# Every two-input operation outside the top-k on VectorE, none of them on GpSimd, in a three-layer fp32 model kernel

## The chip, the core and the metric

One core of one Trainium2 chip runs the whole program in one launch. The time is the device time of one execution in microseconds (us). The kernel before was run three times: 2065.59, 2051.45 and 2052.27 us, median 2052.27. Engines are named as in the profile: PE is TensorE's matrix multiplication, PEld its weight loads, DVE is VectorE, ACT ScalarE, POOL GpSimd, SP the engine whose queue carries the weight transfers.

## The reference, cut to what matters

256 tokens of width 1024 go through one block of three branches with a mixture of experts behind it, and then through two layers of four branches, each with a feed-forward network behind it.

```
# block 1
h = rmsnorm(x, g_mix);  proj = h @ w_in
q_a, k_a, v_a, x_l, gate_l, q_m, gates = split(proj)
attn_out = windowed_gqa(rope(q_a), rope(k_a), v_a, sink)
xc       = conv over 4 tokens of x_l;  lru_out = bidir_rglru(xc, ...) * gelu(gate_l)
            # a = exp(log_a);  bx = sqrt(1 - a*a) * (i * xc);  two scans
mem_out  = memory_cross_attention(q_m, rmsnorm(mem, g_mem) @ w_mem_kv)
merged   = sum over the 3 branches of sigmoid(gates) * (branch @ p)
x = x + merged @ w_out
x = x + peer_ffn(rmsnorm(x, g_ffn))          # scores, two top-16, experts
# two layers, each
h = rms_norm(x, norm1_g);  z = h @ w_in
y0 = retention(z[..])          # q and k rotated: q*cos + turned(q)*sin
y1 = conformer_conv(z[..])     # 31 taps over the tokens, layer norm, silu
y2 = spatial_gating(z[..])     # gelu, layer norm (*g, +b), (w_s * mask) @ v + b_s, times u
y3 = swa_attention(z[..])
x = x + (sum over the 4 of sigmoid(gate) * (y @ w_branch)) @ w_out
x = x + ffn(rms_norm(x, norm2_g))
# at the end rmsnorm with g_final for block 1's part; all in float32
```

## The kernel before, in words

**Weights.** All weights are packed in one stream, in the order of use. A slot of the stream is 8 blocks of 128x128. `Stream._slot` (lines 77 to 101) takes the next slot: for every second one SP issues a transfer of 16 blocks into one of two buffers (`raw`), ACT writes the high half of the slot (`whi`, line 93), and DVE subtracts it from the weights, which gives the low half (`wlo`, line 96). There are 677 slots; in the stretch of the top-k, 59 of the subtractions run on POOL (`pool_share`). Slots have three buffers, so the halves can run at most some two slots ahead of PE. The scheduler gives these operations a high priority.

**Products.** Each block feeds three matmuls (`mm3`, lines 178 to 180, and `mm3a`, lines 184 to 186, where the activations stand still): high by high, high by low, low by high. An activation tile is cut in the same way by `split` (lines 188 to 196: high half by ACT on line 191, low half on line 192).

**The steps that the change touches.** `norm_split` multiplies eight pieces of 128x256 by the norm's factor (`nh`, line 312) and splits each; the low half `hl` goes to POOL for pieces 2, 4 and 6. It is used by six norms on the main path and by the norm of the memory (its names in the trace: `t<-nh,t`). The conv over four tokens (lines 466 to 475) has six pieces whose low halves POOL makes (`t<-t,t`). `lru` squares `lA` (line 564) and multiplies `lX` by `lV` (line 572) on POOL. `gated` (lines 611 to 637) adds a branch for each of eight column groups: a gate product (`gth`, line 634) on DVE, then the addition to `mg` (line 635), on POOL for the middle branches and on DVE for the last. The rotations of the retention end with an addition on POOL (line 1308), the spatial gating with the addition of line 1402 and the product of line 1415, and its weights are masked on POOL (line 1388).

**What sets the order.** Beside the stream of matmuls run background steps (attention, the conv, the recurrence, the retention, the gating). They are generators that are moved on by one step with each pair of blocks of the stream; their matmuls stand between the others. The scheduler places every instruction by its own estimate of times, once, when the program is built. On the chip each engine then works through its fixed list in order: an instruction that waits holds back all behind it on the same engine. So a waiting DVE instruction holds back the next `wlo`, and a late `wlo` holds back PE. The 31 taps of the conv in the two layers (line 1160, `t<-up,hw,t`, 120 for a layer) are filled in after `wlo` operations.

Of the kernel before, what the change touches and what calls it, by code (L numbers as in the profile page):

```python
# [19 lines left out]
P = 128  # L20
# [112 lines left out]
class Core:  # L133
# [174 lines left out]
    def norm_split(self, x, g, rb, hi, lo):  # L308
        nc = self.nc
        for k in range(KD):  # L310
            h = self.scr("nh")
            nc.vector.scalar_tensor_tensor(out=h, in0=x[:, k, :], scalar=g[:, k:k + 1], in1=rb,
                                           op0=ALU.mult, op1=ALU.mult)
            last = self.split(hi[:, k, :], lo[:, k, :], h, eng=nc.vector if k in (0, 1, 3, 5, 7) else nc.gpsimd)
        return last

    def residual(self, w, nk, hi, lo, raw, g):
# [103 lines left out]
    def block1(self):  # L421
        tc, nc, a, ws = self.tc, self.nc, self.a, self.ws
        with ExitStack() as st:
# [42 lines left out]
            def conv():  # L466
                for j in range(6):
                    nc.vector.tensor_scalar(out=xc[:, j, :], in0=xl[:, j, 0:S], scalar1=cw[:, j:j + 1],
                                            scalar2=cb[:, j:j + 1], op0=ALU.mult, op1=ALU.add)
                    for i in range(1, 4):  # L470
                        nc.vector.scalar_tensor_tensor(out=xc[:, j, :], in0=xl[:, j, i:i + S],
                                                       scalar=cw[:, i * 6 + j:i * 6 + j + 1], in1=xc[:, j, :],
                                                       op0=ALU.mult, op1=ALU.add)
                    self.split(xch[:, j, :], xcl[:, j, :], xc[:, j, :], eng=nc.gpsimd)
                    yield 1
            t_conv = self.add(conv())

# [63 lines left out]
            def lru():  # L541
                for j in range(0, 6, 2):
                    A = p.tile([P, 2, 2, S], F32, tag="lA", name="lA", bufs=1)
                    V = p.tile([P, 2, 2, S], F32, tag="lV", name="lV", bufs=1)
                    X = p.tile([P, 2, 2, S], F32, tag="lX", name="lX", bufs=1)
                    for d in range(2):
                        for m in range(2):
                            ps = self.mm.tile([P, 2, S], F32, tag="mm", name="mm")
                            for g in range(2):
                                wh, wl = ws.blks(("lru", 0, 0), d * 6 + j + m, g)  # L550
                                self.mm3(ps[:, g, :], wh, wl, xch[:, j + m, :], xcl[:, j + m, :], True, True)
                            i = d * 6 + j + m
                            col = slice(i, i + 1)
                            th = p.tile([P, 2, S], F32, tag="b2", name="lth", bufs=3)
                            nc.scalar.activation(out=th[:, 0, :], in_=ps[:, 0, :], func=AF.Tanh, scale=0.5,
                                                 bias=self.hbr[:, col])
                            nc.scalar.activation(out=th[:, 1, :], in_=ps[:, 1, :], func=AF.Tanh, scale=0.5,
                                                 bias=self.hbi[:, col])
                            nc.scalar.activation(out=A[:, d, m, :], in_=th[:, 0, :], func=AF.Exp,
                                                 scale=self.nhc[:, col], bias=self.nhc[:, col])  # L560
                            nc.scalar.activation(out=th[:, 0, :], in_=th[:, 0, :], func=AF.Tanh, scale=self.hc[:, col],
                                                 bias=self.hc[:, col])
                            v = V[:, d, m, :]
                            nc.gpsimd.tensor_tensor(out=v, in0=A[:, d, m, :], in1=A[:, d, m, :], op=ALU.mult)
                            nc.vector.scalar_tensor_tensor(out=v, in0=v, scalar=1.0, in1=th[:, 0, :],
                                                           op0=ALU.add, op1=ALU.mult)
                            nc.vector.scalar_tensor_tensor(out=X[:, d, m, :], in0=th[:, 1, :], scalar=1.0,
                                                           in1=xc[:, j + m, :], op0=ALU.add, op1=ALU.mult)
                        yield LRU_PACE
                    for d in range(2):  # L570
                        nc.scalar.activation(out=V[:, d], in_=V[:, d], func=AF.Sqrt, scale=0.25, bias=self.tiny)
                        nc.gpsimd.tensor_tensor(out=X[:, d], in0=X[:, d], in1=V[:, d], op=ALU.mult)
                    yield 2
                    for d in range(2):
                        rev = slice(None, None, -1) if d else slice(None)
                        for m in range(2):
                            nc.vector.tensor_tensor_scan(out=V[:, d, m, rev], data0=A[:, d, m, rev],
                                                         data1=X[:, d, m, rev], initial=0.0, op0=ALU.mult, op1=ALU.add)
                    nc.vector.tensor_tensor(out=V[:, 0], in0=V[:, 0], in1=V[:, 1], op=ALU.add)
                    nc.vector.tensor_tensor(out=V[:, 0], in0=V[:, 0], in1=gl[:, j:j + 2, :], op=ALU.mult)  # L580
                    if j == 0:
                        self.dump("lru", V[:, 0, 0, :])
                    self.split(lh[:, j:j + 2, :], ll[:, j:j + 2, :], V[:, 0])
                    yield 1
# [28 lines left out]
    def gated(self, wg, wp, nk, bh, bl, mg, gh, gl, hgb, first, last, tasks):  # L613

        nc, ws = self.nc, self.ws
        for c in range(KD):
            pg = self.mm.tile([P, S], F32, tag="mm", name="pg")
            for k in range(KD):
                wh, wl = ws.blks(wg, k, c)
                self.mm3(pg, wh, wl, self.hh[:, k, :], self.hl[:, k, :], k == 0, k == KD - 1)  # L620
            th = self.scr("gth")
            nc.scalar.activation(out=th, in_=pg, func=AF.Tanh, scale=0.5,
                                 bias=hgb[:, c:c + 1] if hgb is not None else 0.0)
            if c == 0:
                self.finish(*tasks)
            pp = self.mm.tile([P, S], F32, tag="mm", name="pp")
            for k in range(nk):
                wh, wl = ws.blks(wp, k, c)
                self.mm3(pp, wh, wl, bh[:, k, :], bl[:, k, :], k == 0, k == nk - 1)
            if first:  # L630
                nc.vector.scalar_tensor_tensor(out=mg[:, c, :], in0=th, scalar=1.0, in1=pp,
                                               op0=ALU.add, op1=ALU.mult)
            else:
                nc.vector.scalar_tensor_tensor(out=th, in0=th, scalar=1.0, in1=pp, op0=ALU.add, op1=ALU.mult)
                (nc.vector if last else nc.gpsimd).tensor_tensor(out=mg[:, c, :], in0=mg[:, c, :], in1=th,
                                                                 op=ALU.add)
            if last:
                self.split(gh[:, c, :], gl[:, c, :], mg[:, c, :], scale=0.5)

# [451 lines left out]
    def mixers(self, l):  # L1091
        tc, nc, a, ws = self.tc, self.nc, self.a, self.ws
        with ExitStack() as st:
# [206 lines left out]
            def rot(dst):  # L1300
                r = tmp([P, 2, S], "w2", 7)
                for o, i in ((0, 64), (64, 0)):
# [2 lines left out]
                                            op=ALU.mult)  # L1305
                nc.vector.tensor_tensor(out=dst, in0=dst, in1=cl[:, None, L_COS:L_COS + S].to_broadcast([P, 2, S]),
                                        op=ALU.mult)
                nc.gpsimd.tensor_tensor(out=dst, in0=dst, in1=r, op=ALU.add)
                return
                yield  # L1310

# [73 lines left out]
            def ev_gu(c, ps):  # L1385
                nc.scalar.activation(out=gu[:, c:c + 2, :], in_=ps, func=AF.Gelu_apprx_tanh)
            self.finish(*loads[3])
            nc.gpsimd.tensor_tensor(out=wst, in0=wst, in1=cl[:, None, L_TRI:L_TRI + P].to_broadcast([P, 4, P]),
                                    op=ALU.mult)
            gv = T4().rearrange("p a b -> p (a b)").rearrange("p (t c) -> p t c", t=2)  # L1390
            eh, el = T4(F32R), T4(F32R)
# [4 lines left out]
            def gmlp():  # L1396
                for t in range(2):
                    mv = self.ln_stats(p, [gv[:, t, :]])
                    nc.vector.tensor_scalar(out=gv[:, t, :], in0=gv[:, t, :], scalar1=mv[:, 0, 0:1],
                                            scalar2=mv[:, 0, 1:2], op0=ALU.subtract, op1=ALU.mult)  # L1400
                    nc.vector.tensor_tensor(out=gv[:, t, :], in0=gv[:, t, :], in1=lng[:, 0, :], op=ALU.mult)
                    nc.gpsimd.tensor_tensor(out=gv[:, t, :], in0=gv[:, t, :], in1=lng[:, 1, :], op=ALU.add)
                yield 4
                for g in range(0, 4, 2):
                    ps = self.bg.tile([P, 2, S], F32, tag="bg", name="psg")
                    for i in range(2):
                        for t in range(2):
# [4 lines left out]
                                            in0=ps.rearrange("p a (t q) -> p a t q", t=2),  # L1412
                                            in1=bs[:, g * P:g * P + 2 * P].rearrange("p (a q) -> p a q", a=2)[:, :, None, :]
                                            .to_broadcast([P, 2, 2, P]), op=ALU.add)
                    nc.gpsimd.tensor_tensor(out=y, in0=y, in1=gu[:, g:g + 2, :], op=ALU.mult)
                    self.split(eh[:, g:g + 2, :], el[:, g:g + 2, :], y)
                    yield 1
            self.proj_b(W2["gu"](l), 4, KD, hh, hl, ev_gu)
# [231 lines left out]
```

## Time and profile before

| what | value |
|---|---|
| runs | 2065.59, 2051.45, 2052.27 us; median 2052.27 |
| profiled execution | 2051.29 us, its span 2049.5 us, mean granted TensorE clock 0.993 |
| PE busy | 2006.7 us of the span (98%) |
| DVE busy | 1673.3 us (82%), 3281 instructions |
| ACT busy | 1159.0 us (57%) |
| POOL busy | 277.9 us (14%), 173 instructions |

Of the profiled execution, 2049.5 us lie between the first and the last instruction and 1.8 us around them. PE is idle for 2049.5 - 2006.7 = 42.8 us in all. Engine time that POOL loses or gains has no weight by itself; what counts is what DVE and PE wait for. A row of the waits names the waiting engine with its output and line, then what it waited for, then the total in us, the number of times and the longest. In a row of the timeline, the first number is the start in us, the second the time of the instruction, and since instructions of DVE overlap a little at their ends, the step from one start to the next is what an instruction takes of the engine.

### The profile page before, as it was taken

To read this page: it belongs to the slowest core of one execution; us is meant where nothing else is said; L and a number is where in the kernel's file an instruction comes from. 1 tells how busy PE (TensorE), PEld (TensorE's weight loads), DVE (VectorE), ACT (ScalarE), POOL (GpSimd) and SP (SyncE) were. 2 spreads that over 40 slices of the span, in tenths; PEclk is the share of its full clock that TensorE was granted. 3 is DMA by queue.
4 is the path that set the end of the run, shared out by engine and by line. 5 is a ranking of instruction groups with operands and counts; after the bars stand their busy time and mean duration, and the time that the engine had idled before them with its cause. 6 is when DMAs were issued, how large, how long until landed. Compare 5 with 4: busy or idle time off the path is not lost.

```text
span 2049.5 us, 41488 instructions
## 1 busy us (share of the span) xinstructions
PE 2006.7 (98%) x16818; PEld 1952.2 (95%) x16818; DVE 1673.3 (82%) x3281; ACT 1159.0 (57%) x1906; POOL 277.9 (14%) x173
## 2 busy tenths in 40 slices
PE   8999999999999999989999999999999999999999
PEld 7989999999999999989999889999999989999997
DVE  7877779999999999995568999978555999977554
ACT  6688654445555555544456565566445665466443
POOL 2212207883000000000000101200000101200000
PEclk9999999999999999999999999999999999999999
DMA  5345554454454455454554644555555644554554
GB/s 216 144 133 172 205 205 182 174 197 165 167 183 166 168 184 184 167 184 162 189 195 163 220 162 146 195 195 186 197 194 188 224 158 149 188 188 178 198 195 154
DMA packets 57019, 370.01 MB, mean 181 GB/s; under 512 B 6587, under 2 KB 10236, under 8 KB 13564
## 3 DMA queue, kind: packets, MB, share of 16 engines
q1 hardware_dynamic: 50256, 357.06, 48.4%
q10 hardware_dynamic: 6572, 10.31, 1.7%
q8 instruction: 131, 2.15, 0.4%
q14 instruction: 60, 0.49, 0.1%
HBM read 364.73 MB, written 2.62 MB: 179 GB/s over the span
## 4 chain that ended last, share of the span: by engine, by line
PE 68%; DVE 19%; issue 2%; ACT 2%; DMA 1%; ACTq 0%; DVEq 0%
PE acc L178 5%; PE acc L179 5%; PE acc L180 5%; PE mm L178 5%; PE mm L179 5%; PE mm L180 5%; PE pu L180 3%; PE pu L178 3%; PE pu L179 3%; PE pg L180 3%; PE pg L178 3%; PE pg L179 3%; DVE wlo L96 3%; PE pp L180 2%; PE pp L179 2%
## 5 line engine op out<-in xcount | busy, mean ns | idle before, releaser
L93 ACT ACTIVATE whi<-raw 128x1024 fp32r<-128x1024 f32 x677 | 717.5, 1061 | 738.7 <-DMA raw<-in_w 166.1
L96 DVE TENSOR_TENSOR wlo<-raw,whi 128x1024 fp32r<-128x1024 f32 x618 | 765.6, 1240 | 308.7 <-ACT whi L93 306.5
L180 PE MATMUL pu<-hh,wlo 128*128 128x256 f32 x1024 | 286.5, 280 | 2.1 <-POOL wlo L96 2.1
L178 PE MATMUL pu<-hh,whi 128*128 128x256 f32 x1024 | 285.2, 278 | 1.1 <-ACT whi L93 1.1
L180 PE MATMUL mm<-hh,wlo 128*128 128x256 f32 x1008 | 280.7, 279 | 5.1 <-DVE wlo L96 5.0
L179 PE MATMUL pu<-hl,whi 128*128 128x256 f32 x1024 | 283.8, 277 | 0.0
L178 PE MATMUL mm<-hh,whi 128*128 128x256 f32 x1008 | 281.0, 279 | 0.0
L179 PE MATMUL mm<-hl,whi 128*128 128x256 f32 x1008 | 280.4, 278 | 0.0
L178 PE MATMUL acc<-ga,whi 128*128 128x256 f32 x1000 | 277.4, 280 | 2.3 <-ACT ga L191 2.3
L179 PE MATMUL acc<-ga,whi 128*128 128x256 f32 x1000 | 277.5, 278 | 1.1 <-DVE ga L192 1.1
L180 PE MATMUL acc<-ga,wlo 128*128 128x256 f32 x1000 | 276.6, 278 | 0.0
L180 PEld LDWEIGHTS mm<-hh,wlo 128*128 128x128 f32 x1008 | 190.2, 189 | 8.1 <-DVE wlo L96 6.9
L178 PE MATMUL pg<-hh,whi 128*128 128x256 f32 x704 | 197.3, 280 | 0.0
L180 PE MATMUL pg<-hh,wlo 128*128 128x256 f32 x704 | 196.6, 279 | 0.5 <-DVE wlo L96 0.5
L179 PE MATMUL pg<-hl,whi 128*128 128x256 f32 x704 | 196.4, 279 | 0.0
L180 PEld LDWEIGHTS pu<-hh,wlo 128*128 128x128 f32 x1024 | 193.1, 189 | 2.3 <-POOL wlo L96 2.3
L178 PEld LDWEIGHTS pu<-hh,whi 128*128 128x128 f32 x1024 | 193.3, 189 | 1.7 <-ACT whi L93 1.5
L179 PEld LDWEIGHTS pu<-hl,whi 128*128 128x128 f32 x1024 | 193.1, 189 | 0.0
L178 PEld LDWEIGHTS mm<-hh,whi 128*128 128x128 f32 x1008 | 190.3, 189 | 1.4 <-issue 0.7
L179 PEld LDWEIGHTS acc<-ga,whi 128*128 128x128 f32 x1000 | 189.8, 190 | 1.3 <-DVE ga L192 1.3
L179 PEld LDWEIGHTS mm<-hl,whi 128*128 128x128 f32 x1008 | 190.0, 189 | 1.1 <-issue 0.8
L178 PEld LDWEIGHTS acc<-ga,whi 128*128 128x128 f32 x1000 | 188.1, 189 | 2.6 <-ACT ga L191 2.6
(413 smaller groups left out, 4901.3 us busy)
## 6 DMA issues: line engine op xcount, KB each, us to landing
raw<-in_w SPq DMA_DIRECT2D x336, 1024.0 KB
raw<-in_w SPq DMA_DIRECT2D x5, 512.0 KB
bias<-bias_scr ACTq DMA_DIRECT2D x4, 512.0 KB
bias_scr<-sbb ACTq DMA_DIRECT2D x16, 96.0 KB
cl<-in_cstl ACTq DMA_DIRECT2D x2, 576.0 KB
x<-in_xT SPq DMA_DIRECT2D x4, 256.0 KB
memt<-in_memT ACTq DMA_DIRECT2D x1, 1024.0 KB
keys<-in_keysT ACTq DMA_DIRECT2D x1, 1024.0 KB
```

The source lines that it names most:

```text
L93: self.on_scalar = nc.scalar.activation(out=hi, in_=src, func=AF.Copy).ins
L96: i = eng.tensor_tensor(out=lo, in0=src, in1=hi.bitcast(F32), op=ALU.subtract)
L178: mm(out, lhsT=wh, rhs=xh, start=start, stop=False)
L179: mm(out, lhsT=wh, rhs=xl, start=False, stop=False)
L180: self.on_pe = mm(out, lhsT=wl, rhs=xh, start=False, stop=stop).ins
```

## The change

All two-input operations named above go from POOL to DVE: 103 instructions, 79 of 128x256 (40 additions to `mg`, 18 low halves `hl` of the main norms, 3 of the memory's norm, 6 of the conv, 12 squares) and 24 of 128x512 (8 of line 1308, 6 of line 572, 4 each of lines 1402 and 1415, 2 of line 1388). POOL keeps the 59 `wlo` of the top-k and a few small operations. From `gated` on, the changed kernel's line numbers are one lower. The whole diff, with the context cut:

```diff
@@ norm_split
-            last = self.split(hi[:, k, :], lo[:, k, :], h, eng=nc.vector if k in (0, 1, 3, 5, 7) else nc.gpsimd)
+            last = self.split(hi[:, k, :], lo[:, k, :], h)
@@ conv of block 1
-                    self.split(xch[:, j, :], xcl[:, j, :], xc[:, j, :], eng=nc.gpsimd)
+                    self.split(xch[:, j, :], xcl[:, j, :], xc[:, j, :])
@@ lru
-                            nc.gpsimd.tensor_tensor(out=v, in0=A[:, d, m, :], in1=A[:, d, m, :], op=ALU.mult)
+                            nc.vector.tensor_tensor(out=v, in0=A[:, d, m, :], in1=A[:, d, m, :], op=ALU.mult)
...
-                        nc.gpsimd.tensor_tensor(out=X[:, d], in0=X[:, d], in1=V[:, d], op=ALU.mult)
+                        nc.vector.tensor_tensor(out=X[:, d], in0=X[:, d], in1=V[:, d], op=ALU.mult)
@@ gated
-                (nc.vector if last else nc.gpsimd).tensor_tensor(out=mg[:, c, :], in0=mg[:, c, :], in1=th,
-                                                                 op=ALU.add)
+                nc.vector.tensor_tensor(out=mg[:, c, :], in0=mg[:, c, :], in1=th, op=ALU.add)
@@ rot
-                nc.gpsimd.tensor_tensor(out=dst, in0=dst, in1=r, op=ALU.add)
+                nc.vector.tensor_tensor(out=dst, in0=dst, in1=r, op=ALU.add)
@@ spatial gating
-            nc.gpsimd.tensor_tensor(out=wst, in0=wst, in1=cl[:, None, L_TRI:L_TRI + P].to_broadcast([P, 4, P]),
+            nc.vector.tensor_tensor(out=wst, in0=wst, in1=cl[:, None, L_TRI:L_TRI + P].to_broadcast([P, 4, P]),
                                     op=ALU.mult)
...
-                    nc.gpsimd.tensor_tensor(out=gv[:, t, :], in0=gv[:, t, :], in1=lng[:, 1, :], op=ALU.add)
+                    nc.vector.tensor_tensor(out=gv[:, t, :], in0=gv[:, t, :], in1=lng[:, 1, :], op=ALU.add)
...
-                    nc.gpsimd.tensor_tensor(out=y, in0=y, in1=gu[:, g:g + 2, :], op=ALU.mult)
+                    nc.vector.tensor_tensor(out=y, in0=y, in1=gu[:, g:g + 2, :], op=ALU.mult)
```

Since the scheduler places everything anew, other instructions of DVE change places too. Three places follow.

The first is DVE in the opening of block 1, where the taps of the conv over four tokens (line 471) run beside the first weights; `angn` is made from the positions, which a transfer brings. Before:

```order
L471 SCALAR_TENSOR_TENSOR t_496<-xl,par,t_496 128x256 x3
L731 TENSOR_SCALAR sp<-sp 128x12
L471 SCALAR_TENSOR_TENSOR t_496<-xl,par,t_496 128x256 x4
L732 RECIPROCAL sp<-sp 128x12
L692 CAST angn<-pos 32x256
L96 TENSOR_TENSOR wlo<-raw,whi 128x1024
```

And in the changed kernel:

```order
L471 SCALAR_TENSOR_TENSOR t_496<-xl,par,t_496 128x256 x3
L730 TENSOR_SCALAR sp<-sp 128x12
L471 SCALAR_TENSOR_TENSOR t_496<-xl,par,t_496 128x256 x3
L691 CAST angn<-pos 32x256
L471 SCALAR_TENSOR_TENSOR t_496<-xl,par,t_496 128x256
L731 RECIPROCAL sp<-sp 128x12
L471 SCALAR_TENSOR_TENSOR t_496<-xl,par,t_496 128x256
L96 TENSOR_TENSOR wlo<-raw,whi 128x1024
```

Between the operation on the positions and the `wlo` behind it now stand two taps and a reciprocal.

The second is DVE at the norm of the memory (`nh<-memt`), which runs beside the rotation of block 1's queries (`ropet`, `kt`, `t_499`). Before:

```order
L96 TENSOR_TENSOR wlo<-raw,whi 128x1024
L192 TENSOR_TENSOR t_834<-nh,t_833 128x256 x3
L312 SCALAR_TENSOR_TENSOR nh<-memt,par,rb 128x256
L743 SCALAR_TENSOR_TENSOR hc<-sp 128x12
L312 SCALAR_TENSOR_TENSOR nh<-memt,par,rb 128x256
L491 TENSOR_TENSOR ropet<-pr,rsin 32x512
L96 TENSOR_TENSOR wlo<-raw,whi 128x1024
L312 SCALAR_TENSOR_TENSOR nh<-memt,par,rb 128x256
L96 TENSOR_TENSOR wlo<-raw,whi 128x1024
```

And in the changed kernel:

```order
L96 TENSOR_TENSOR wlo<-raw,whi 128x1024
L192 TENSOR_TENSOR t_834<-nh,t_833 128x256
L493 TENSOR_TENSOR t_499<-t_499,ropet 32x512
L192 TENSOR_TENSOR t_834<-nh,t_833 128x256 x3
L742 SCALAR_TENSOR_TENSOR hc<-sp 128x12
L96 TENSOR_TENSOR wlo<-raw,whi 128x1024
L192 TENSOR_TENSOR t_834<-nh,t_833 128x256
L312 SCALAR_TENSOR_TENSOR nh<-memt,par,rb 128x256
L491 TENSOR_TENSOR ropet<-pr,rsin 32x512
L312 SCALAR_TENSOR_TENSOR nh<-memt,par,rb 128x256 x2
L96 TENSOR_TENSOR wlo<-raw,whi 128x1024
```

The pieces of `nh` that reuse buffers have moved behind the first `wlo`, and the low halves made by POOL before now stand in DVE's list.

The third is DVE in the first of the two layers, where the retention's group statistics (`BN_STATS` of `py`) are due and the taps of the conv (`t_14797<-up,hw`) run between. Before:

```order
L96 TENSOR_TENSOR wlo<-raw,whi 128x1024
L1160 SCALAR_TENSOR_TENSOR t_14797<-up,hw,t_14797 128x256
L192 TENSOR_TENSOR t_14805<-po,t_14804 64x2x128
L1160 SCALAR_TENSOR_TENSOR t_14797<-up,hw,t_14797 128x256
L1448 BN_STATS s_15845<-py 128x6 x4
```

And in the changed kernel:

```order
L96 TENSOR_TENSOR wlo<-raw,whi 128x1024
L192 TENSOR_TENSOR t_14805<-po,t_14804 64x2x128
L1159 SCALAR_TENSOR_TENSOR t_14797<-up,hw,t_14797 128x256
L1344 TENSOR_TENSOR rsc<-prs,cl 128x256
L1345 TENSOR_TENSOR rsc<-prs,cl 128x128
L1159 SCALAR_TENSOR_TENSOR t_14797<-up,hw,t_14797 128x256 x7
L192 TENSOR_TENSOR t_14805<-po,t_14804 64x2x128
L1159 SCALAR_TENSOR_TENSOR t_14797<-up,hw,t_14797 128x256
L1447 BN_STATS s_15845<-py 128x6 x2
```

In both kernels the next `wlo` stands only behind all the statistics; from the `wlo` shown to that one, two taps stood in the list before and ten stand there now, with a pair of score products (`rsc`), a low half and a gate product more.

## Rows read from the trace of the kernel before

**Rows 1.** The page: busy us, share of the span and instructions.

```profile
PE 2006.7 (98%) x16818; PEld 1952.2 (95%) x16818; DVE 1673.3 (82%) x3281; ACT 1159.0 (57%) x1906; POOL 277.9 (14%) x173
```

**Rows 2.** Waits of PE: waited for, total us, times, longest.

```profile
PE mm L180 <- DVE wlo L96: 5.0, 5, 2.0
PE mm L186 <- DVE wlo L96: 4.1, 5, 1.2
PE mml L179 <- DVE hl L192: 2.0, 3, 1.1
```

**Rows 3.** Windows: us, busy PE, PEld, DVE, ACT, POOL (instructions), clock, DMA.

```profile
110.00:240.00 130.00, 127.03 (x991) 121.15 (x991) 96.16 (x187) 106.57 (x189) 27.52 (x26) 1.00 0.49 165
1140.00:1240.00 100.00, 97.18 (x690) 86.33 (x689) 97.32 (x193) 61.76 (x117) 8.49 (x5) 1.00 0.46 165
1240.00:1345.00 105.00, 104.99 (x905) 104.60 (x905) 96.83 (x161) 61.20 (x92) 21.71 (x20) 1.00 0.51 180
```

**Rows 4.** POOL by line: busy us, mean ns; idle before, and its releaser.

```profile
L635 POOL TENSOR_TENSOR mg<-mg,gth 128x256 f32<-128x256 f32 x40 | 41.5, 1038 | 137.5 <-DVE gth L634 137.5
L192 POOL TENSOR_TENSOR hl<-nh,hh 128x256 fp32r<-128x256 f32 x18 | 19.8, 1109 | 410.7 <-ACT hh L191 410.7
L1308 POOL TENSOR_TENSOR t<-t,w 128x512 f32<-128x512 f32 x8 | 14.2, 1774 | 61.0 <-DVE t L1306 50.8 <-DVE sm L1263 5.8 <-DVE sm L1265 4.3
L192 POOL TENSOR_TENSOR t<-t,t 128x256 fp32r<-128x256 f32 x6 | 12.6, 2128 | 12.6 <-ACT t L191 12.6
L564 POOL TENSOR_TENSOR lV<-lA 128x256 f32<-128x256 f32 x12 | 8.7, 734 | 84.9 <-ACT lA L559 76.1 <-DVE t L192 8.9
L1402 POOL TENSOR_TENSOR t<-t,lng 128x512 f32<-128x512 f32 x4 | 8.1, 2016 | 118.6 <-DVE t L1401 118.6
L572 POOL TENSOR_TENSOR lX<-lX,lV 128x512 f32<-128x512 f32 x6 | 7.7, 1288 | 18.5 <-ACT lV L571 18.5
L1388 POOL TENSOR_TENSOR wst<-wst,cl 128x512 f32<-128x512 f32 x2 | 3.6, 1798 | 58.4 <-DMA wst<-in_gmlp_wsT 58.4
```

**Rows 5.** Timeline of DVE, a 512-wide product and the next start.

```profile
1248.22 0.68 DVE L1401 TENSOR_TENSOR t<-t,lng 128x512 f32<-128x512 f32 x1
1248.81 1.22 DVE L96 TENSOR_TENSOR wlo<-raw,whi 128x1024 fp32r<-128x1024 f32 x1
```

**Rows 6.** Timelines of DVE and POOL, an addition of line 635.

```profile
1301.52 0.42 DVE L634 SCALAR_TENSOR_TENSOR gth<-gth,pp 128x256 f32<-128x256 f32 x1
1301.85 0.48 DVE L1160 SCALAR_TENSOR_TENSOR t<-up,hw,t 128x256 f32<-128x256 f32 x1
1302.26 1.76 DVE L96 TENSOR_TENSOR wlo<-raw,whi 128x1024 fp32r<-128x1024 f32 x1
...
1302.02 0.92 POOL L635 TENSOR_TENSOR mg<-mg,gth 128x256 f32<-128x256 f32 x1 [3.94 <-DVE gth L634]
```

**Rows 7.** Timeline of DVE, first and last lengthened instruction outside the top-k.

```profile
26.92 0.63 DVE L192 TENSOR_TENSOR hl<-nh,hh 128x256 fp32r<-128x256 f32 x1
...
1882.49 1.02 DVE L312 SCALAR_TENSOR_TENSOR nh<-x,par,rb 128x256 f32<-128x256 f32 x1
```

**Rows 8.** Timeline of DVE, opening: the operation on the positions, the `wlo` behind.

```profile
37.88 0.28 DVE L692 CAST angn<-pos 32x256 f32<-32x256 int32 x1 [0.79 <-DMA pos<-in_positions]
38.08 1.20 DVE L96 TENSOR_TENSOR wlo<-raw,whi 128x1024 fp32r<-128x1024 f32 x1
```

**Rows 9.** Timelines of DVE and POOL, the memory's norm.

```profile
79.09 0.95 DVE L312 SCALAR_TENSOR_TENSOR nh<-memt,par,rb 128x256 f32<-128x256 f32 x1 [0.64 <-POOL t L192]
...
74.76 5.00 POOL L192 TENSOR_TENSOR t<-nh,t 128x256 fp32r<-128x256 f32 x2 [19.49 <-ACT t L191]
```

**Rows 10.** Windows of PE alone: us, PE busy, granted clock, DMA.

```profile
80.00:82.00 2.00, 0.28 (x3) 1.00 0.76 320
82.00:84.00 2.00, 1.71 (x11) 0.76 0.00 0
84.00:86.00 2.00, 2.00 (x11) 0.50 0.41 115
```

## The prediction, made before the changed kernel was run

> **What bounds the kernel now.** I read the page's busy line first. PE is busy 2006.7 us of the span of 2049.5 us [rows 1], so only 42.8 us of idle PE can be won at all, and DVE at 82% has room as a mean. Next come PE's waits, to see how much of that idle time hangs on what the change touches: the low halves of the weights, `wlo`, for 5.0 and 4.1 us, and low halves of activations in the norms' first matmuls for 2.0 us [rows 2]; 11.1 us together. Most of the rest is the start, the expert part and waits for ACT, which the change does not touch. POOL's own results hardly appear in that list, so POOL's slowness costs PE nothing directly.
>
> Then the stages, since the mean of DVE misleads. In the recurrence's stretch (110 to 240 us) DVE is busy 96.16 of 130 us; in the first half of a layer's mixers 97.32 of 100, and in the gated sums behind it 96.83 of 105 [rows 3]. The second layer looks alike. In the mixers DVE has almost no room, yet PE loses only about 3 us of 100 there. So this is decided on DVE: what leaves it, what comes to it, and in which order it meets the `wlo`.
>
> **What POOL costs DVE today.** An addition on POOL of 0.92 us starts at 1302.02, and the `wlo` that DVE starts at 1302.26 takes 1.76 us [rows 6] where the same operation takes 1.22 us alone [rows 5]: 0.54 us longer. Outside the top-k I count 62 such lengthened rows of DVE, from 26.92 us (0.63 where the one before it takes 0.42) to 1882.49 us (1.02 where 0.47 is usual) [rows 7], 34.05 us over all of them: 3.8 before 110 us, 2.3 in the recurrence, 12.6 and 11.3 in the two layers' mixers, about 1 at each of four norms. All of this goes, since no POOL operation is left there.
>
> **What the change adds to DVE.** 79 operations of 128x256 and 24 of 128x512. The step from one start to the next is 0.33 us for a 256-wide one (1301.52 to 1301.85 [rows 6], the nearest row of that shape) and 0.59 us for a 512-wide one [rows 5]; I take 0.60. That is 79 x 0.33 + 24 x 0.60 = 26.1 + 14.4 = 40.5 us, against 34.05 freed: 6.5 us more of DVE, of 376 idle. By stage:
> - a layer's mixers get 16 additions of line 635 and 4 + 2 + 2 + 1 wide ones, 16 x 0.33 + 9 x 0.60 = 10.7 us, and free 12.6 or 11.3: even, or slightly better;
> - the opening gets 12 x 0.33 = 4.0 and frees 3.8: even;
> - the recurrence gets 12 squares, 6 wide products and 8 additions, 20 x 0.33 + 6 x 0.60 = 10.2, frees 2.3: 7.9 us more, which makes 104 of 130. Cover is the 34 us that DVE idles there;
> - the norms get 3 x 0.33 each and free about as much: nothing, except before the expert part.
>
> The POOL times that go, 41.5 for line 635 and 19.8 for the norms' halves with them [rows 4], were beside the path and are worth nothing by themselves.
>
> **Where it meets the path.** The sum, against the profiled execution of 2051.3 us:
> 1. *Weights in the mixers.* Of the 9.1 us, 5.6 lie in seven gaps of 0.5 to 1.2 us in the two layers' first halves. There the rotation's sum, 1.8 us on POOL [rows 4] beside DVE, no longer lengthens `wlo`. Adding steps along both lists, DVE reaches most of these `wlo` 1 to 2 us earlier. Bounds: 0 (the time goes to other work of DVE) and -5.6. I take -3.0, about the middle.
> 2. *Opening.* DVE waits for the positions until 37.88 and then makes the `wlo` on which PE waits 1.2 us [rows 2, 8]. Two taps and a reciprocal now stand between: 2 x 0.41 (a tap's step, 1301.85 to 1302.26 [rows 6]) + 0.1 = +0.9. The gap becomes 2.1 us. Behind the longest `wlo` gap now, 2.0 us, the granted clock falls to 0.76 and 0.50 of full speed [rows 10], that is to the 1.2 GHz level for a time; (0.24 + 0.50) x 2 us = 1.5 us lost. Behind the gap of 1.2 us it stays at 1.00. So a gap of 2.1 should cost the 1.5 too: +2.4. Bounds: 0 (the positions land earlier than the taps) and +2.4.
> 3. *The memory's norm.* Here the reverse. DVE waits 0.64 us for a buffer that POOL holds through two halves of 5.00 us, and then its row is lengthened by about half a us [rows 9]: 1.1 us go, one low half more (0.33) comes. The gap of 2.0 us [rows 2] shrinks to about 1.2 and its slow clock goes: -0.8 - 1.5 = -2.3. Bounds: 0 and -3.5.
> 4. *Retention.* Between two `wlo` around the group statistics eight taps more have gathered, 8 x 0.41 = 3.3 us, with about 1.0 of other work. The scheduler spent the room it saw there. The `wlo` run at most two slots ahead of PE, which covers most of it. Bounds 0 and +2.5 a layer; I take +0.6 each, +1.2.
> 5. *Recurrence.* `lV` and `lX` now wait on DVE for ACT, in front of `wlo`. POOL idled 18.5 us over six for line 571 [rows 4], 3 us each. That is the upper end if none is hidden, so 0 to +18; with DVE idle a quarter of the stretch I take +0.5. The squares wait for ACT's exponential in the same way and are in that figure.
> 6. *Norm before the expert part.* Three halves come into a stretch where DVE is full: 0 to 1.0, I take +0.5.
> 7. *Mask of the gating weights.* It waited for a transfer on POOL (58.4 us of idle [rows 4]) and now stands on DVE before the rotation. By the landing times DVE gets there at most 0.4 us early: 0. *Rotations, gating, gated sums* have no other price than the DVE time above: their results come earlier, 0.6 us instead of 1.8 to 2.0 [rows 4, 5].
>
> Sum: -3.0 + 2.4 - 2.3 + 1.2 + 0.5 + 0.5 = -0.7, so 2050.6 for an execution like the profiled one. The median shown, 2052.27, lies 1.0 above that one; I forecast **2051.5**, with a range of its own of 2044 to 2058 (terms 1, 3 at one end, terms 2, 4, 5 at the other). A change of under 1%, 20.5 us, is what I call none.
>
> **Rivals.**
> *Late weights with a slow clock (ends slower).* The retention's gathered taps are not hidden: in each layer a `wlo` comes 2.5 us late, and such a gap is followed by the half clock, as at 82 us [rows 10]. That is 2 x (2.5 + 1.5) = 8.0 in place of term 4, with term 1 gone as the late work eats it: -0.7 + 8.0 - 1.2 + 3.0 = +9.1, 2060.4, by the median 2061.5. It decides from a gap of about 2 us. For it: the ten taps in a row of the list, and 97.32 of 100 us [rows 3]. Against it: the two slots of lead.
>
> *DVE becomes the bound in the mixers (slower by 1%).* The lengthening does not come off as time, because DVE's list waits on other things; then 10.7 us a layer come on top: 2 x 10.7 = 21.4, 2073.7. For it: DVE is at 97% there. Against: the lengthened rows are measured and POOL has nothing left to lengthen them with.
>
> *POOL blocks more than the rows show (faster).* If a POOL operation holds DVE for its whole time, every late low half that hangs on DVE vanishes: -(5.0 + 4.1 + 2.0) - 1.5 = -12.6, so 2038.7, by the median 2039.7. For it: the 0.54 us lie near the 0.68 us that were left of the addition when the `wlo` began. Against: the moved operations take far more on POOL, 41.5 us for line 635 alone [rows 4], than DVE loses, 34.05 for all. The Trainium skill, "SBUF — State Buffer", section "SBUF: two separate sides", says that a GpSimd operation and a DVE operation with two SBUF inputs take a shared pair of ports as an exclusive lock for the whole instruction, and that the one which comes second is fully blocked. The trace agrees in the one row and does not in the total. By that rule the sum would be this rival's, by the rows it is mine.
>
> That the work stays on POOL is excluded: its list keeps only the `wlo` of the top-k and small ones.
>
> **Chances.** The forecast 0.59, late weights 0.24, the blocking rival 0.09, DVE as the bound 0.08. The range of 8 in 10 reaches from 2040 (the blocking rival's place) to 2064 (the late weights with the upper end of term 5 in part). Left out are DVE as the bound, 0.08, and some 0.1 of tails. Faster by over 1% (under 2031.7) needs half of all idle time of PE, more than every wait for DVE holds: 0.02. Slower by over 1% (over 2072.8): DVE as the bound in most of its cases, 0.07. Within 1%: 0.91.
>
> **What would show it.** `wlo` outside the top-k never over 1.3 us; POOL busy near 150 us (277.9 less the moved operations), DVE near 1680 (1673.3 + 6.5). PE's waits for `wlo` in the first halves of the layers under 3 us; a gap near 39 us of about 2.1 with a clock under 1.00 behind it; none at 82 us. At the retention's statistics no gap over 1 us. Wrong would be: gaps of 2 us or more in the mixers with a clock of 0.5 behind them, DVE rows that wait for ACT's `lV` with PE idle behind, or a PE whose idle time falls by 10 us and more.

## The result, and the profile after

The changed kernel takes 2076.26 us (median of 8 runs, 2066.46 to 2082.34). The kernel before, run beside it, has by now a median of 2059.09 (8 runs, 2051.45 to 2065.59): the ratio is 1.0078, with an interval of 1.0051 to 1.0105. So the change costs some 17 us. The forecast was 2051.5 in a range of 2040 to 2064. Part of that distance has nothing to do with the change: two of the three runs shown before, their median and the profiled one with them, were at the fast end of what the kernel before does (2051.45 and 2052.27 of 2051.45 to 2065.59).

The page of the changed kernel begins with the busy line, which answers to [rows 1]:

```profile
PE 2028.0 (98%) x16818; PEld 1972.3 (95%) x16818; DVE 1682.0 (81%) x3384; ACT 1166.8 (56%) x1910; POOL 144.2 (7%) x70
```

DVE grew by 8.7 us, where 6.5 was worked out, and POOL lost 133.7. But PE is busy 21.3 us longer with the same 16818 matmuls, and its idle time went from 42.8 to 2076.5 - 2028.0 = 48.5 us. Both are looked into below.

The groups of DVE and POOL show that the prices were right. The columns are those of [rows 4].

```profile
L96 DVE TENSOR_TENSOR wlo<-raw,whi 128x1024 fp32r<-128x1024 f32 x618 | 753.2, 1221 | 319.2 <-ACT whi L93 314.3 <-PE pu L180 1.5 <-PE pg L180 0.7
L635 DVE TENSOR_TENSOR mg<-mg,gth 128x256 f32<-128x256 f32 x64 | 26.9, 420 | 0.8
L1307 DVE TENSOR_TENSOR t<-t,w 128x512 f32<-128x512 f32 x8 | 5.4, 680 | 0.0
```

The `wlo` on DVE take 1221 ns on the mean and 1246 at most, so they are no longer lengthened; an addition to `mg` takes 420 ns where POOL took 1038, a rotation's sum 680 where it took 1774.

The waits of PE answer to [rows 2]:

```profile
PE pp L178 <- ACT t L194: 8.3, 2, 4.6
...
PE pt L248 <- DVE apr L663: 4.2, 3, 1.7
PE mm L180 <- DVE wlo L96: 3.2, 4, 1.7
...
PE pg L178 <- ACT gth L622: 1.9, 2, 1.6
...
PE mml L179 <- DVE hl L192: 1.4, 3, 1.0
...
PE mm L186 <- DVE wlo L96: 0.2, 1, 0.2
```

The two rows of waits for `wlo` that [rows 2] shows fell from 9.1 to 3.4 us together. In their place stands one that the kernel before does not have at all: 8.3 us in two waits, for a tile that ACT's line 194 writes. Line 194 is the scaled split, and `pp` with it is the first product of the last branch in a layer, so this is the end of the conv with 31 taps. The three waits for `apr` are block 1's attention softmax.

Where the conv was ready in the kernel before, in the first layer, the timelines of DVE, ACT and PE show in turn: its last two taps, the second half of its split, and PE's first product with it.

```profile
1315.11 0.99 DVE L1160 SCALAR_TENSOR_TENSOR t<-up,hw,t 128x256 f32<-128x256 f32 x2
...
1339.65 0.70 ACT L194 ACTIVATE t<-t 128x512 fp32r<-128x512 f32 x1
...
1340.68 0.28 PE L178 MATMUL pp<-t,whi 128*128 128x256 f32 x1
```

The split ends at 1340.35 and PE arrives at 1340.68. There were 0.33 us of slack (0.32 in the second layer), and no view of waits shows a slack. The same three places in the changed kernel, where other work runs 14 to 15 us later by then:

```profile
1336.62 1.53 DVE L1159 SCALAR_TENSOR_TENSOR t<-up,hw,t 128x256 f32<-128x256 f32 x3
...
1358.54 0.63 ACT L194 ACTIVATE t<-t 128x512 fp32r<-128x512 f32 x1 [0.37 <-DVE t L1187]
...
1359.23 0.58 PE L178 MATMUL pp<-t,whi 128*128 128x256 f32 x1 [4.56 <-ACT t L194]
```

The last tap ends 22.1 us later than before, the split 18.8 us later, and PE, which could have gone on at 1354.67, waits 4.56 us. In DVE's list the last tap stood behind the `wlo` of slot 425 in the first layer and 585 in the second; in the changed kernel it stands behind 428 and 588. A `wlo` cannot run before its slot's buffer is free, so three slots in the list, at 24 matmuls of 0.113 us each, are 8.1 us on the clock, however fast DVE is. Some 3 of these 8 us are made up between the last tap and the split; the rest is the 0.33 us of slack and PE's wait. The wait is followed by the lower clock level; these are windows of PE alone, as in [rows 10]:

```profile
1358.00:1360.00 2.00, 0.77 (x3) 0.67 0.75 315
1360.00:1362.00 2.00, 2.00 (x12) 0.50 0.00 0
1362.00:1364.00 2.00, 2.00 (x19) 0.98 0.00 0
```

(0.33 + 0.50 + 0.02) x 2 = 1.7 us are lost behind it, and as much behind the wait in the second layer. So the conv's lateness costs 8.3 + 3.4 = 11.7 us in this profile. In each of the other three profiles of the changed kernel, the lower level lasted 6.8 us instead of 3.4 at one of the two waits, so the cost is about 1 us higher there.

And the time that DVE won? The windows of the recurrence and of a layer's two halves, shifted to where they lie now, answer to [rows 3]:

```profile
110.00:240.00 130.00, 125.08 (x949) 118.87 (x948) 101.69 (x210) 105.35 (x186) 0.00 (x0) 0.99 0.48 156
...
1155.00:1255.00 100.00, 99.06 (x699) 87.85 (x698) 94.28 (x191) 63.42 (x116) 0.00 (x0) 1.00 0.47 164
1255.00:1360.00 105.00, 98.31 (x858) 97.70 (x857) 97.36 (x186) 61.43 (x91) 0.00 (x0) 0.99 0.51 181
```

In the first half of the mixers PE gained 2 us, and DVE has 3 us of idle time more than it had; in the second half DVE is as full as ever and PE loses 6.7 of 105 us.

### The profile page after: what moved, and what is told of

Read it like the earlier page. It is cut to its first block, busy times and chain, and to the rows that moved or that the text cites. A ratio compares the mean times of both kernels' runs of the same rounds, so it can differ in the third digit from the quotient of the medians.

```text
span 2076.5 us, 41409 instructions
## 1 busy us (share of the span) xinstructions
PE 2028.0 (98%) x16818; PEld 1972.3 (95%) x16818; DVE 1682.0 (81%) x3384; ACT 1166.8 (56%) x1910; POOL 144.2 (7%) x70
## 4 chain that ended last, share of the span: by engine, by line
PE 77%; DVE 16%; ACT 4%; issue 2%; DMA 1%; ACTq 0%; SPq 0%; DVEq 0%
PE mm L178 7%; PE mm L180 7%; PE mm L179 7%; PE acc L178 6%; PE acc L179 6%; PE acc L180 5%; PE pg L178 3%; PE pg L179 3%; PE pg L180 3%; PE pu L180 3%; PE pu L178 3%; PE pu L179 3%; DVE wlo L96 2%; PE mm L184 2%; PE mml L178 2%; PE mm L186 2%
## 5 line engine op out<-in xcount | busy, mean ns | idle before, releaser
L96 DVE TENSOR_TENSOR wlo<-raw,whi 128x1024 fp32r<-128x1024 f32 x618 | 753.2, 1221 | 319.2 <-ACT whi L93 314.3
L178 PE MATMUL pu<-hh,whi 128*128 128x256 f32 x1024 | 288.0, 281 | 0.6 <-ACT whi L93 0.6
L178 PE MATMUL mm<-hh,whi 128*128 128x256 f32 x1008 | 281.7, 280 | 0.2 <-ACT whi L93 0.2
L178 PE MATMUL acc<-ga,whi 128*128 128x256 f32 x1000 | 279.2, 282 | 2.3 <-ACT ga L191 2.3
L178 PE MATMUL pg<-hh,whi 128*128 128x256 f32 x704 | 199.2, 283 | 2.4 <-ACT gth L622 1.9
L178 PEld LDWEIGHTS pu<-hh,whi 128*128 128x128 f32 x1024 | 193.1, 189 | 1.0 <-ACT whi L93 0.8
L178 PEld LDWEIGHTS acc<-ga,whi 128*128 128x128 f32 x1000 | 189.5, 191 | 2.6 <-ACT ga L191 2.6
L178 PEld LDWEIGHTS mm<-hh,whi 128*128 128x128 f32 x1008 | 189.4, 188 | 2.2 <-issue 1.3
```

The source lines that it names most:

```text
L96: i = eng.tensor_tensor(out=lo, in0=src, in1=hi.bitcast(F32), op=ALU.subtract)
L178: mm(out, lhsT=wh, rhs=xh, start=start, stop=False)
```

## Experiments

Each kernel was run beside the kernel before on one chip. Beside the additions to mg on GpSimd, the three taps everywhere and the first repetition of the two kernels, the kernel before had a median of 2058.97 (25 runs); beside the other four versions, on another chip, 2057.18 (29 runs). Two kinds of theory were there at the start. *Late conv*: the list has the last taps later, and PE waits. *Rivals*: DVE's added work counts as a whole, or the step from matmul to matmul is what changed, since the two traces showed stretches at 113.3 ns and at 117.8 ns a step, with more of the latter after the change.

**One part undone: the additions to mg stay on GpSimd.**

```diff
-                nc.vector.tensor_tensor(out=mg[:, c, :], in0=mg[:, c, :], in1=th, op=ALU.add)
+                (nc.vector if last else nc.gpsimd).tensor_tensor(out=mg[:, c, :], in0=mg[:, c, :], in1=th, op=ALU.add)
```

> The change with one part undone: the additions to mg (line 635) of the middle branches stay on GpSimd, 40 instructions; all else is on DVE. In DVE's list the last tap of the conv stands behind slot 426 and 585 (before 425 and 585, changed 428 and 588). Late conv: PE's waits at the first product of the last branch go, with the half clock behind them, so some 10 us less than the changed kernel, 2064 to 2068, and DVE rows are lengthened again in the gated sums (16 to 20 us). Rival (all of DVE's added work counts, in proportion): 40 x 0.33 = 13.2 of 40.5 us go, a third of the 17 us, 2070. Rival (step level alone): no difference beyond chance, 2076.

Measured: 2062.65, ratio to before 1.0026 (1.0006 to 1.0046). The wait for the conv is gone, and the time is just under the expected range. 14 us came back, not the third that the work's share would give, so the rival of DVE's added work falls; it is somewhat more than the 11.7 us of the late conv. It also shows what moved the taps: with the additions to `mg` alone put back on GpSimd, the last taps stand behind slots 426 and 585 again.

**Three taps a step everywhere.**

```diff
-TAPS = 2
+TAPS = 3
```

> The whole change, with three taps of the conv for each step of its background work instead of two; nothing else is changed. The last tap stands in DVE's list behind slot 418 and 579, ten slots (some 27 us) earlier than in the changed kernel. Late conv: the waits at the first product of the last branch are gone, 8.3 us, and the half clock behind them, 3.4 us: 2064 to 2066. Against it, DVE has more taps in front of the first halves' weights: waits of PE for wlo there could come back, up to 5.6 us as in the kernel before. Rival (step level, or DVE's work as a whole): 2076, as the changed kernel, since DVE has the same work.

Measured: 2073.53, ratio 1.0074 (1.0045 to 1.0103). Only 3 us came back where 10 to 12 were expected. The wait for the conv is gone, but the earlier taps now stand in between the steps of the sliding attention's softmax (lines 1261 to 1271), and other waits of PE came in its place:

```profile
PE pp L178 <- ACT gth L622: 4.5, 4, 1.7
PE po L1285 <- ACT w L1281: 4.2, 2, 3.5
PE pt L248 <- DVE apr L663: 4.2, 3, 1.6
PE ptt L248 <- DVE t L1271: 3.3, 3, 1.9
```

The second and fourth are that softmax's, the first is for the gates; the three are 12.0 us, as much as the late conv had cost with its clock. (The third is block 1's and was there before this edit.)

**Three taps a step in the later half of the conv alone.**

```diff
-                        if i % TAPS == 0:
+                        if i % (3 if j >= 2 else TAPS) == 0:
```

> The whole change, with three taps instead of two for each step of the conv's background work, but only in the third and fourth of its four channel groups. The last tap stands behind slot 425 and 586 in DVE's list, as in the kernel before (changed: 428 and 588), while the first half of the taps stays where the change has it. Late conv: the waits at the first product of the last branch (8.3 us and 3.4 for the clock) go, and nothing comes in front of the attention's softmax as it did with three taps everywhere: 2063 to 2067. Rival (DVE's work as a whole, or step level): 2076.

Measured: 2066.31, ratio 1.0036 (1.0012 to 1.0059), as late conv said. The wait for the conv is gone from the rows of PE's waits: its split is ready 2.5 us before PE in the first layer and 0.25 in the second. So with all 103 instructions on DVE, some 10 us of the loss go when the last taps stand where they stood before, though the edit moves other instructions of the lists too. Some 7 to 9 us against the kernel before stay.

**The kernel before with a later conv, no work moved to DVE.**

```diff
-            t_conv = self.add(conv(bh, bl))
+            t_conv = self.add(conv(bh, bl), 4)
```

> The kernel before, all its operations on GpSimd as they were, with one number changed: the conv's background work in the two layers starts three steps later. The last tap stands behind slot 428 and 588 in DVE's list, as in the changed kernel. Late conv: what costs is the place of the last tap in the list and not DVE's work, so PE waits 3 to 6 us at the first product of the last branch in each layer, with half clock behind: +8 to +13, 2067 to 2072. Rival (DVE's added work): nothing is added, 2059.

Measured: 2078.68, ratio 1.0110 (1.0076 to 1.0144), more than expected. Its waits of PE:

```profile
PE pp L178 <- ACT t L194: 12.0, 2, 6.0
PE pu L178 <- ACT whi L93: 7.6, 2, 6.7
...
PE pg L178 <- ACT gth L622: 2.4, 1, 2.4
```

Twice 6.0 us for the conv, and some 3.4 more for the half clock behind, 1354.8 to 1358.0 and 1832.4 to 1835.9 us. So without one instruction more on DVE, a conv that stands later in the list costs some 15 us, nearly as much as the whole change. The other 6 of the 21 us are not the conv's. The 6.7 us for `whi` lie in the expert part at 486 us, far from what was edited; in the four profiles of the kernel before that row reads 0.6 to 2.8 us in all. Whether it comes with every execution of this kernel was not tried, and so it is open why its median went above the expectation.

**The two layers' part alone, and block 1 and the norms alone.** In the first, lines 635 (of the layers), 1308, 1388, 1402 and 1415 go to DVE, in the second all others:

```diff
@@ layers alone
-                (nc.vector if last else nc.gpsimd).tensor_tensor(out=mg[:, c, :], in0=mg[:, c, :], in1=th,
+                (nc.vector if last or hgb is None else nc.gpsimd).tensor_tensor(out=mg[:, c, :], in0=mg[:, c, :], in1=th,
...
-                nc.gpsimd.tensor_tensor(out=dst, in0=dst, in1=r, op=ALU.add)
+                nc.vector.tensor_tensor(out=dst, in0=dst, in1=r, op=ALU.add)
...
@@ block 1 and norms alone
+                (nc.vector if last or hgb is not None else nc.gpsimd).tensor_tensor(out=mg[:, c, :], in0=mg[:, c, :], in1=th,
...
+            last = self.split(hi[:, k, :], lo[:, k, :], h)
...
```

> Only the two layers' parts of the change (32 additions to mg, rotations, gating, mask: 50 of the 103 instructions) go to DVE; block 1 and all norms stay as before. The last tap of the conv stands behind slot 428 and 587 in DVE's list, as in the changed kernel. Late conv: PE waits 4 to 5 us at the first product of the last branch in each layer, with half clock behind, so +9 to +13 us over the kernel before, 2068 to 2072. Rival (DVE's added work in proportion): 21.4 of 40.5 us, +9, but without these waits. Rival (block 1 is where it went): 2059, no change.

> Only block 1's parts and all norms' low halves go to DVE (8 additions to mg, 27 low halves, 12 squares, 6 products: 53 instructions); the two layers keep theirs on GpSimd. The last taps stand behind slot 425 and 585, as before. Late conv: no wait at the last branch, at most a few us over the kernel before, 2057 to 2064. Rival (block 1 is where it went): +10 or more, 2069 and up. Rival (the added DVE work in proportion): 19 of 40.5 us, +8, 2067.

Measured: the layers alone 2069.41, ratio 1.0059 (1.0032 to 1.0086); block 1 and the norms alone 2062.36, ratio 1.0019 (0.9997 to 1.0041). 12.2 and 5.2 us add up to the 17 of the whole, but the interval of the second includes no change. The wait for the conv is there in the first only, and only in the first layer:

```profile
PE pp L178 <- ACT t L194: 4.3, 1, 4.3
```

So for the layers alone the forecast time came out, but only in part by the forecast way: one wait of 4.3 us, with 5.8 us of half clock behind it, is about 7 of the 12 us. In the second layer, with the last tap behind slot 587, the split was ready just as PE came. That profile also has 4.2 us of waits for ACT's gates (`gth`), where the kernel before has 0.2 at most. In block 1's kernel the softmax waits stand, as in the changed one:

```profile
PE pt L248 <- DVE apr L664: 4.2, 3, 1.6
```

**The same two kernels again, for the step of the matmuls.**

> The kernel before once more, unchanged, for a second profile of the same list. In the first profile the matmuls of the stream step by 113.3 ns in most stretches and by 117.8 ns in others (some 280 us at the higher level before, some 760 us after the change); 23 groups of 8 slots were 0.85 us longer after the change, some 18 of the 27 us between the two traces. If the level is set anew in each execution, the stretches at 117.8 ns lie elsewhere here, and their sum may be several 100 us (a time of up to 2065). If the program sets it, they lie at the same places and sum to 280 us again. Time: the same as the kernel before, 2051 to 2066 us.

> The changed kernel once more, unchanged. Theory (late conv): PE waits at the first product of the last branch, for the conv's last split, 4.6 and 3.7 us, each with 3.4 us of half clock behind (1.7 us lost), in this profile too, within 1 us, since the list makes it: 11.7 us of the change's some 17. Rival (the step of the matmuls, 113.3 or 117.8 ns, is what the change moved): the stretches at 117.8 ns lie at the same places as in the first profile and sum to some 760 us. If they are accidental, their sum differs by 100 us or more from the first profile's. Time 2066 to 2082 us, ratio to before about 1.008.

> The kernel before, unchanged, for a third profile. In two profiles of it the stream's matmuls stepped by 117.8 ns for 278 and 346 us (together with the changed kernel's 758 and 767 this would be 0.038 x 450 = 17 us). If the program sets this, the third lies at 250 to 400 us; if each execution sets it, it may lie anywhere from 250 to 800.

> The kernel before, unchanged, for a fourth profile: as for the third, 250 to 400 us at 117.8 ns if the program sets it, anywhere from 250 to 800 if each execution does.

> The changed kernel, unchanged, for a third profile. If the program sets the step, 700 to 850 us at 117.8 ns; if each execution sets it, anywhere from 250 to 800. The waits at the first product of the last branch are 4.6 and 3.7 us again (late conv).

> The changed kernel, unchanged, for a fourth profile: as for the third, 700 to 850 us at 117.8 ns if the program sets it, anywhere from 250 to 800 if each execution does; the waits at the last branch stay at 4.6 and 3.7 us.

The two medians: before 2057.79 (ratio 0.9988, 0.9963 to 1.0013), after 2076.62 (ratio 1.0091, 1.0057 to 1.0124). The step is settled by windows of PE over stretches where all is weights and no wait stands: 720 to 900 us (a part of the experts) and 950 to 1090 us. The kernel before, first, third and fourth profile:

```profile
720.00:900.00 180.00, 180.00 (x1669) 1.00 0.49 177
950.00:1090.00 140.00, 140.00 (x1238) 1.00 0.54 195
```

```profile
720.00:900.00 180.00, 180.00 (x1610) 1.00 0.49 175
950.00:1090.00 140.00, 140.00 (x1192) 1.00 0.51 184
```

```profile
720.00:900.00 180.00, 180.00 (x1668) 1.00 0.50 178
```

And the changed kernel, first and second:

```profile
720.00:900.00 180.00, 180.00 (x1666) 1.00 0.50 181
950.00:1090.00 140.00, 140.00 (x1191) 1.00 0.52 185
```

```profile
720.00:900.00 180.00, 180.00 (x1614) 1.00 0.51 176
950.00:1090.00 140.00, 140.00 (x1237) 1.00 0.55 196
```

In 140 us at a granted clock of 1.00, PE does 1238 matmuls or 1192, with one and the same program, in either kernel. The third and fourth profiles of both kernels were taken on another chip than the second ones, so a difference between the early and the late ones could be the chip's. But the third and fourth of the kernel before, on one chip, differ too: 1610 against 1668 matmuls in the 180 us from 720 us on. So each execution sets the step anew, stretch by stretch; whether the chip has a part in it was not tried. Over all steps of the stream, counted one by one, the time above 113.3 ns is 10.6, 13.8, 27.1 and 25.3 us in the four profiles of the kernel before, and 28.8, 28.2, 29.9 and 24.6 in those of the changed one. At 4.5 ns a step that is, as an estimate, 280, 360, 710 and 660 us at 117.8 ns before and 750, 740, 780 and 640 after. The third and fourth of the kernel before leave the 250 to 400 us that the program would have set, and the last of the changed kernel leaves its 700 to 850. The first two of the changed kernel have nearly the same sum, but at different places. The first profile, on which the prediction was built, is the lowest of all. The waits for the conv, in contrast, were 8.3 us in all four of the changed kernel.

| profile | span | PE busy | PE idle | clock |
|---|---|---|---|---|
| before, first to fourth | 2049.5, 2055.4, 2067.1, 2061.0 | 2006.7, 2012.2, 2024.0, 2019.6 | 42.8, 43.2, 43.1, 41.4 | 0.993, 0.992, 0.994, 0.995 |
| after, first to fourth | 2076.5, 2080.8, 2083.8, 2074.4 | 2028.0, 2031.3, 2034.1, 2023.8 | 48.5, 49.5, 49.7, 50.6 | 0.993, 0.990, 0.990, 0.993 |

By their means the spans differ by 20.6 us: 7.0 of idle PE, some 4.3 of half clock (0.0065 of 2058 us against 0.0085 of 2079), and 8.7 of longer steps. The first two come from the lists. The third comes out of four executions each of something that varied by 16 us in one and the same kernel; whether the changed program draws long steps more often, or these four did by chance, stays open. The third and fourth profiles, on one chip, are the nearest to a fair pair, since their long steps are about equal (26.2 us on the mean before, 27.3 after). Their spans differ by 15.1 us: 7.9 of idle PE, some 6.3 of half clock and 1.1 of steps. In the first and second the spans differ by 26.2 us, and 16.3 of these are steps. The medians put the whole at 17 to 19 us, so some 6 us are not assigned by the means of all eight, and some 3 to 5 by the late pair.

No version that was run beats the kernel before.

## Why the prediction was wrong

**The work and its prices** held: 8.7 us more of DVE against 6.5, POOL at 144.2 against about 150, no lengthened `wlo`. The DVE time that came free is 40.5 - 8.7 = 31.8 us, against 34.05.

**"A layer's mixers ... even, or slightly better"** is the step that failed. It added up what DVE gains and loses in us, and took time won as time that any work of DVE can use. A list does not allow that. The taps stand between `wlo`, a `wlo` goes at the pace of PE, and the new list has the last taps three slots further back. What DVE won in the first half it idled away in front of the weights; the taps at the end came 8 us late all the same. The third place shown in the section on the change had the ten taps gathered at the retention, but they were followed only to the next `wlo`. The end of the same taps, and the product of PE that waits for it, is missing from the sum: term 7 says that the gated sums "have no other price than the DVE time above", and there 8.3 us of waits came, with 3.4 us or more lost to the half clock behind them. With these came the prediction's own sign of being wrong: gaps of 2 us or more in the mixers with a clock of 0.5 behind. The two slot numbers in the lists and the 0.33 us of slack in the trace before were there to be read.

**Term 1, weights in the mixers**, -3.0: too small, in the right direction. Six gaps in the first halves sum to 5.1 us (the seventh, 0.5, stands in the second layer's gated sums and in another row), and of these 0.2 are left in the row of line 186. Some 0.9 us of waits for `whi` came there instead (0.3 before, 1.2 now). PE gained 1.9 us in the window of the first layer.

**Term 2, the opening**, +2.4. The wait for the positions is there, and the `wlo` behind it starts at 38.20 with two taps between:

```profile
37.12 0.28 DVE L691 CAST angn<-pos 32x256 f32<-32x256 int32 x1 [1.06 <-DMA pos<-in_positions]
37.33 0.47 DVE L471 SCALAR_TENSOR_TENSOR t<-xl,par,t 128x256 f32<-128x256 f32 x1
37.73 0.21 DVE L731 RECIPROCAL sp<-sp 128x12 f32<-128x12 f32 x1
37.87 0.40 DVE L471 SCALAR_TENSOR_TENSOR t<-xl,par,t 128x256 f32<-128x256 f32 x1
38.20 1.20 DVE L96 TENSOR_TENSOR wlo<-raw,whi 128x1024 fp32r<-128x1024 f32 x1
```

PE's wait grew from 1.2 to 1.7 us instead of 2.1, since the positions landed 0.8 us sooner. The half clock followed in only one of the four profiles (the third), so the term is +0.5 in this one and not +2.4.

**Term 3, the memory's norm**, -2.3: the gap of 2.0 us at 82 us became one of 0.5, less than the 1.2 forecast, and its half clock is gone. But a half clock came at 116 us instead, with the waits of term 5.

**Term 5, the recurrence**, +0.5: too small. With block 1's operations on DVE, the order of the softmax beside them changed (the same waits stand in block 1's kernel alone, and not in the layers'). Three waits follow each other between 111 and 116 us, 3.2 us in all, where before there was one of 1.5, and the clock falls behind them, in windows of PE alone:

```profile
112.00:114.00 2.00, 0.33 (x1) 1.00 0.00 0
114.00:116.00 2.00, 1.02 (x5) 1.00 0.45 78
116.00:118.00 2.00, 2.00 (x9) 0.56 0.97 410
118.00:120.00 2.00, 2.00 (x8) 0.59 0.11 41
```

With a third wait for `apr` at 181 us, PE is busy 125.08 of the 130 us instead of 127.03: 1.9 us of waits more, and 1.7 of clock in place of the 1.7 at 82 us. DVE's `lX` waited for ACT for 3.7 us over five times, and no wait of PE stands behind it.

**Term 4, the retention**, +1.2: no `wlo` was late there. PE waited 1.6 us in the first layer and 0.3 in the second for ACT's gate instead, the row `PE pg L178 <- ACT gth L622` above. In the first layer, ACT's square root for the late statistics had itself waited 1.31 us for DVE at 1254 us. So the size, 1.9 us, came near by luck.

**Term 6, the norm before the expert part**, +0.5: no wait of PE over 0.1 us is left there except the 1.3 us for `ld`, which is the same before and after. **Term 7**, the mask: as forecast, DVE does not wait for the transfer there.

**The rivals.** "Late weights with a slow clock" had the right kind of mechanism: one late item of DVE's list in each layer, a wait of some us, the half clock behind. It had the wrong item, and its 2061.5 was too low. "DVE becomes the bound" has the nearest number, 2073.7, by luck: PE's waits for `wlo` fell, and with all of the work still on DVE some 10 us came back when the last taps stood earlier. "POOL blocks more" falls as far as busy times show: 31.8 us of DVE's came free, near the 34.05 of the lengthened rows and far from the 133.7 that POOL lost. On the rule of the Trainium skill, "SBUF — State Buffer", section "SBUF: two separate sides", these runs decide nothing more: with no GpSimd operation beside it a `wlo` takes 1.22 us, which either of the two readings gives.

**The base.** 2052.27 was the median of three runs, and the profile was of a run with few long steps. Against the 2059 of more runs the forecast of "no change" would have been 2058, inside the range that it had, with the change still some 18 above.

## What to carry to other kernels

Where lists are fixed when a program is built, time won on an engine is worth something only where the list lets the late work move up. So compare positions and not only sums: for each result that the bounding engine takes from the edited engine, count behind which paced instruction its producer stands before and after, and read in the trace how much slack it had. And before a fraction of a per cent is forecast from one profile, see how much two executions of the same kernel differ.

## What the runs showed of the hardware

In stretches without a wait and at a granted clock of 1.00, the stream's 128x256 matmuls step by 113.3 or by 117.8 ns, for 100 us and more at a time, and the same program has the one or the other at the same place in different executions (1238 against 1192 matmuls in 140 us). Over the four profiles of the kernel before, from at least two chips, this made a difference of up to 16 us. What picks the level was not found. The half clock followed the opening's wait of 1.9 us in the third profile of the changed kernel and not that of 1.7 us in the first; and a row of three waits of 1.3, 1.2 and 0.7 us at 112 us was followed by it where a single wait of 1.5 us there, in the kernel before, was not.
